# Bulk loads of adjacent rows, and bulk results that leave in runs of 8 bytes instead of 32

## The chip, the cores and the metric

One Trainium2 chip, one core in use. The metric is the device time of one execution in microseconds (us); medians of several executions are given. In the profile a packet is one unbroken run of bytes that one of the core's 16 DMA engines moves. A pitch is the distance in memory from one partition's piece to the next one's. A store's receipt is the time from its last packet to its landing.

## The reference

For a float32 matrix of 8192 x 8192 (268 MB) the largest absolute value of each row:

```python
def reference(x):                       # x: 8192 x 8192 float32
    return np.linalg.norm(x, ord=np.inf, axis=1)
```

Every element is read once and compared once; the output is 8192 floats, 32 KB. The kernel is therefore a load stream with a reduction behind it.

## The kernel before

The rows are divided into a bulk (48 rows for each of the 128 partitions) and a tail (16 rows for each). In the bulk, each load brings `B` = 2 rows to each partition: 128 x 64 KB = 8 MB. Three buffers take turns.

```python
G: int = 4, B: int = 2, BUFS: int = 3
# ...
A = n_bulk_rows // (G * B)              # 48 // 8 = 6
x_b = x[:split].rearrange("(a p n b) c -> a n p (b c)", p=P, a=A, n=G, b=B)
out_b = out[:split].rearrange("(a p n b) -> p a (n b)", p=P, a=A, n=G, b=B)
# ...
r_bulk = outp.tile([P, A, G * B], F32)
# ...
for a in range(A):
    for n in range(G):
        t = sbuf.tile([P, W + PAD], F32, tag="t")
        nc.sync.dma_start(out=t[:, :W], in_=x_b[a, n])
        absmax(r_bulk[:, a, n * B : (n + 1) * B],
               t[:, :W].rearrange("p (b c) -> p b c", b=B))
# ... the tail: loads of falling size, 21 and then 13, each with its reduction ...
    if j == len(LAST) - 4:              # late in the tail
        ins = nc.scalar.dma_start(out=out_b, in_=r_bulk[:])   # the bulk store
        after(ins, done, mybir.DependencyClass.Sync)
nc.sync.dma_start(out=out_t, in_=r_tail[:])                   # the last store
```

With `G` = 4, a partition owns 8 neighbouring rows in each of 6 groups and reads two of them in each load. Its 8 results are neighbours in the output, so the bulk store moves 128 x 6 = 768 runs of 32 bytes.

## Time and profile before

| | before |
|---|---|
| median time | 627.68 us (627.46 to 627.82, 3 runs) |
| span in the profile | 625.7 us |
| DMA engines | full in all 40 slices but the end |
| last load packet ends | 622.66 us |
| bulk store: issued, landed | 621.73, 623.73 us |
| last store: issued, landed | 624.05, 625.47 us |

"Landed" is the moment at which the store's completion counter has its last increment. The lines themselves stand in the prediction below.

### The profile page before, as it was taken

The numbers are of one execution on the slowest core, as the hardware profiler recorded it, in microseconds if no ns is written. First come the engines' busy times: TensorE is split into PE (matmuls) and PEld (weight loads), VectorE is DVE, ScalarE is ACT, GpSimd is POOL, SyncE is SP. The second block draws the span as 40 slices with busy tenths as digits, with TensorE's granted clock in tenths as the row PEclk, the third lists the DMA queues.
The fourth block names the chain that finished last, engine by engine and source line by source line (L and its number), as shares of the span: only waits on it lengthen the run. The fifth ranks groups of instructions, "written<-read, shape, count | busy, mean of one in ns | idle before, by whom it ended". The sixth has DMA issues, their size and how long they took to land.

```text
span 625.7 us, 205 instructions
## 1 busy us (share of the span) xinstructions
DVE 552.9 (88%) x67; POOL 0.2 (0%) x4
## 2 busy tenths in 40 slices
DVE  0588988889988889888898888988889999999998
POOL 0000000000000000000000000000000000000000
DMA  9999999999999999999999999999999999999997
GB/s 402 469 402 452 419 452 419 448 423 436 436 419 452 411 461 402 469 402 469 402 469 402 461 411 452 419 448 423 444 413 421 444 425 431 436 425 430 424 422 315
DMA packets 9282, 268.49 MB, mean 429 GB/s; under 512 B 1856, under 2 KB 1856, under 8 KB 3392
## 3 DMA queue, kind: packets, MB, share of 16 engines
q1 hardware_dynamic: 8496, 268.45, 99.5%
q10 hardware_dynamic: 784, 0.02, 0.1%
q14 instruction: 2, 0.02, 0.0%
HBM read 268.44 MB, written 0.03 MB: 429 GB/s over the span
## 4 chain that ended last, share of the span: by engine, by line
DMA 67%; DVE 31%; issue 1%; another core or an unknown queue 0%; DVEq 0%; SPq 0%
DMA t<-in_x_dram 67%; DVE r_bulk L140 24%; DVE part L140 6%; DVE t L140 2%; DVEq L230 0%; DVE r_tail L140 0%; SPq L159 0%
## 5 line engine op out<-in xcount | busy, mean ns | idle before, releaser
L140 DVE TENSOR_REDUCE r_bulk<-t 128x2 f32<-128x16384 f32 x24 | 413.3, 17220 | 69.7 <-DMA t<-in_x_dram 69.7
L140 DVE TENSOR_REDUCE part<-t 128x1 f32<-128x8192 f32 (+20 forms) x28 | 121.5, 4410 | 0.3 <-DMA t<-in_x_dram 0.3
L140 DVE TENSOR_REDUCE t<-t 128x1 f32<-128x1664 f32 (+8 forms) x11 | 16.7, 1576 | 0.2 <-DMA t<-in_x_dram 0.2
L140 DVE TENSOR_REDUCE r_tail<-t 128x1 f32<-128x644 f32 (+1 forms) x2 | 1.5, 814 | 0.0
L137 DVE MEMSET part<- 128x56 f32 x1 | 0.1, 105 | 0.9 <-PEq L219 0.9
L140 DVE TENSOR_REDUCE r_tail<-part 128x14 f32<-128x56 f32 x1 | 0.2, 201 | 0.0
L219 POOL MEMSET const-bfloat16-1.0<- 128x1 bf16 x1 | 0.1, 101 | 0.0
L219 POOL MEMSET const-uint8-127<- 128x1 uint8 x1 | 0.1, 101 | 0.0
L219 POOL MEMSET const-float32-0.0<- 128x1 f32 x1 | 0.1, 98 | 0.2 <-issue 0.2
L219 POOL MEMSET const-float32-1.0<- 128x1 f32 x1 | 0.1, 98 | 0.0
## 6 DMA issues: line engine op xcount, KB each, us to landing
t<-in_x_dram SPq DMA_DIRECT2D x2, 3392.0 KB, 37.2
t<-in_x_dram SPq DMA_DIRECT2D x1, 5376.0 KB, 40.5
t<-in_x_dram SPq DMA_DIRECT2D x1, 4864.0 KB, 32.9
t<-in_x_dram SPq DMA_DIRECT2D x1, 4800.0 KB, 32.9
t<-in_x_dram SPq DMA_DIRECT2D x1, 4672.0 KB, 34.7
t<-in_x_dram SPq DMA_DIRECT2D x3, 1536.0 KB, 36.9
t<-in_x_dram SPq DMA_DIRECT2D x1, 3520.0 KB, 42.7
t<-in_x_dram SPq DMA_DIRECT2D x1, 3328.0 KB, 40.4
```

What stands on the lines that cost most here:

```text
L137: nc.vector.memset(part[:], 0.0)
L140: return nc.vector.reduce_max(out=o, in_=i, axis=X, apply_absolute_value=True)
L219: nc = _bacc.Bacc("TRN2", target_bir_lowering=False, num_devices=1)
```

## The change

The intent is to let each bulk load read one unbroken stretch of 8 MB, where before its 128 pieces of 64 KB lay 256 KB apart. The price is in the output: a partition then owns only 2 neighbouring rows in each of 24 groups.

```diff
-    G: int = 4,
+    G: int = 1,
```

So `A` becomes 24, and the bulk store moves 128 x 24 = 3072 runs of 8 bytes. Nothing else changes, neither in the order of instructions nor in their waits.

## The prediction

> **What bounds the kernel now.** I read the page's head and slices first, to see which resource is full; then the same question in equal windows, to see whether it is full in every stage; then the groups of instructions, for what the other engine has to spare; then the chain that ended last and the timeline of the last four microseconds, because the change also touches a store that sits there.
>
> The page of the kernel before, head, slices and queues (share of the span for each engine; tenths busy and GB/s in 40 slices; packets, MB and share of the 16 DMA engines for each queue):
>
> ```profile
> span 625.7 us, 205 instructions
> DVE 552.9 (88%) x67; POOL 0.2 (0%) x4
> ...
> DMA  9999999999999999999999999999999999999997
> ...
> DMA packets 9282, 268.49 MB, mean 429 GB/s; under 512 B 1856, under 2 KB 1856, under 8 KB 3392
> q1 hardware_dynamic: 8496, 268.45, 99.5%
> q10 hardware_dynamic: 784, 0.02, 0.1%
> ```
>
> The DMA engines are full from the first slice to the last; VectorE, the only computing engine, is at 88%. Queue 1 (all loads, and the small last store) takes 99.5% of 16 engines' time. Queue 10 is the bulk store: 784 packets, 24 KB, 0.1%. So the load stream is the bound, and its rate is the question.
>
> The equal windows (us, then VectorE busy, POOL busy, clock, DMA share, GB/s): two in the bulk stage, two in the tail of smaller loads.
>
> ```profile
> 136.00:194.00 58.00, 51.66 (x3) 0.00 (x0) 1.00 1.00 434
> 368.00:426.00 58.00, 51.66 (x3) 0.00 (x0) 1.00 1.00 434
> 500.00:560.00 60.00, 59.71 (x11) 0.00 (x0) 1.00 0.99 427
> 560.00:610.00 50.00, 49.97 (x19) 0.00 (x0) 1.00 1.01 427
> ```
>
> Every 58 us brings three bulk loads, at 434 GB/s, with the DMA engines never idle. VectorE has 58.00 - 51.66 = 6.3 us of slack in each such window, which is the idle time of the first group here:
>
> ```profile
> L140 DVE TENSOR_REDUCE r_bulk<-t 128x2 f32<-128x16384 f32 x24 | 413.3, 17220 | 69.7 <-DMA t<-in_x_dram 69.7
> ```
>
> A reduction takes 17.22 us where a load takes 58.02 / 3 = 19.34 us. In the queue's own waits each of these loads waits for the reduction that frees its buffer (361.6 us over 21 waits), but two loads are always queued ahead, so these waits cost the stream nothing: the DMA share in the windows is 1.00.
>
> The packet records give the rate in its parts. All 3072 bulk packets are 64 KB, one for each partition of each load, at a median of 2418 ns: 65536 / 2418 = 27.1 GB/s for an engine, 434 for 16. Eight packets for each engine in each load make 8 x 2.418 = 19.34 us, exactly the load's period. Small load packets of 2560 bytes take 102 ns. A line through both sizes is 7.8 ns + bytes / 27.2 GB/s, and it also gives the sizes between (26112 bytes: 968 ns both measured and by the line). So the rate of a packet is set by a fixed 27.2 GB/s for an engine and a few ns for each packet.
>
> The end, from the chain that ended last (start, length, what) and from the timeline:
>
> ```profile
> 612.35 9.89 DVE t L140 x8
> 622.25 0.23 issue
> 622.48 0.59 DVE r_tail L140
> ```
>
> ```profile
> 621.73 0.41 ACTq L200 DMA_DIRECT2D out_dram<-r_bulk  x1
> 622.48 1.55 DVE L140 TENSOR_REDUCE r_tail<-t 128x1 f32<-128x644 f32 x2
> 624.05 0.35 SPq L202 DMA_DIRECT2D out_dram<-r_tail  x1
> ```
>
> The last load packet ends at 622.66. The last reduction ends at 624.03, the last store is issued at 624.05, and its packets run from 624.89 to 625.10 in the packet records. The page's list of issues has it landing 1.4 us after issue, at 625.47; the span ends at 625.73. The bulk store is issued at 621.73, its first packet is at 622.69 (after nearly all load packets), its last at 623.21, and it has landed 2.0 us after issue, at 623.73. It is off the end by 625.47 - 623.73 = 1.74 us.
>
> **What the Trainium skill says.** "DMA: Bandwidth & Descriptors", section "Where 436 GB/s comes from", gives 16 ports x 32 bytes x 850 MHz = 435.2 GB/s on the SBUF side. The trace's 434 in the bulk stage is within 0.4% of it, so the case agrees: the ceiling is where the data is written, not in the order in which HBM is read.
>
> The same page, "Latency and other measured facts", reports that copies between HBM tensors slow down at large power-of-two pitches between partitions: 207 GB/s at 512 KiB against 214 at full rate, 164 at 2 MiB. It recommends laying tiles out contiguously. That is the likely intent here. This trace shows no loss to recover: 256 KB pitch in the bulk and 512 KB in the tail (8 segments of 64 KB for each partition) lie on the same line of ns against bytes.
>
> The same page, "Measured (HBM→SBUF, 128 partitions, SWDGE, issued from GpSimd)", puts the smallest packets at about 10.5 ns each. Here the bulk store's 49 packets on an engine took 0.52 us, 10.6 ns each, though on another issuing path.
>
> **The change, part by part.** With G = 1 the number of bulk steps is 48 rows / (1 x 2) = 24 where it was 6 groups of 4. The number of loads, their size, their order on the queue, their waits and the reductions stay: the ordering tool shows no difference on SyncE or VectorE. Two things change.
>
> (1) Load addresses. Each partition still reads one 64 KB run, so packets remain 3072 of 64 KB; only the pitch between partitions falls from 256 KB to 64 KB. By the line above this is worth 0. What could be gained at most: raising 434 to the page's 435.2 over the bulk's 465 us is 465 x 0.0034 = 1.6 us, and about half of the difference is the fixed ns for each packet, which stays; the mean bulk packet is 2422 ns against a median of 2418, so stalls that a better pattern could remove are 4 x 8 x 24 ns = 0.8 us, nearly all of it in the first load (mean 2497 ns), where the start-up is. I count 0, with 0.3 us either way.
>
> (2) The bulk store. Its runs in HBM were 8 results = 32 bytes; they become 2 results = 8 bytes. Packets with data go from 768 to 3072, that is from 48 to 192 for each engine. Added engine time: 144 x 10.8 ns (0.52 us / 48) = 1.56 us. Issue: the store with 48 data packets for an engine took 0.41 us to issue, the last store with 8 took 0.35, so about 1.65 ns for each packet; 144 more make about 0.24 us, of which some may delay the first packet. All this comes after the last loads have been read, so it doesn't delay them. It first fills the slack: last packet at 622.69 + 192 x 0.0108 = 624.77, or 625.01 with the whole issue delay; receipts took 0.35 to 0.51 us after the last packet before, so it lands between 625.1 and 625.5. The last store lands at 625.47 now. So the bulk store arrives just about when the last store does. Where the two overlap (624.89 on), each engine has a few packets more to take turns with, 0.1 to 0.2 us. Sum: 1.56 + 0.24 + 0.2 = 2.0 us of added work, of which 1.74 us is slack; the end moves by 0 to 0.5 us. I take 0.3.
>
> Total: 627.68 + 0 + 0.3 = 628.0 us.
>
> **The rivals.** (a) HBM locality makes the loads faster. For it: adjacent rows, and the skill's advice. Against it: every engine already moves 27.1 GB/s with no idle time. It can give 1 us at most: 626.7.
>
> (b) The adjacent pattern makes the loads slower, because at a 64 KB pitch the engines running in step meet in the same HBM channels. For it: nothing in this trace, only that 64 KB is also a power of two. Against it: 256 and 512 KB show no such loss, and the new pattern as a whole covers one unbroken range. If packets became 1% slower in the bulk, the load stream would add 4.7 us: 632. VectorE's slack means that no second bound appears.
>
> (c) The 8-byte writes cost more than 10.8 ns each, because several partial writes fall into the same line of memory, or because ACT's queue cannot produce descriptors that fast. For it: 32-byte writes had receipts up to 0.51 us after the last packet, 64-byte ones 0.21 to 0.37. Against it: the packets themselves last 7 to 9 ns whatever their size up to 64 bytes. At twice the cost a packet the store would land 2.1 us later than reckoned, near 627.4, and the time would be 629.7.
>
> (d) The store starts earlier and hits the loads. It cannot: its wait, on the reduction before it, is not moved.
>
> **Range and chances.** The step from which the range comes is (2): from nothing visible (627.3, with the usual scatter of 0.2 us and a trace of (a)) to a store half again as slow (629.3). A change by 2% is 12.6 us. Up, it needs packets of the bulk 2.7% slower, which only (b) gives; down, it would need more than 435 GB/s. Chances: faster 0.01, same 0.97, slower 0.02.
>
> **What would show it.** In the changed kernel's page: 11586 packets in all (9282 + 2304), those of queue 10 3088 where 784 were; the bulk windows again 58 us for three loads at 434 GB/s; 64 KB packets again at 2418 ns; the bulk store landing about 3.5 us after its issue (2.0 + 1.56) and the last store still 1.4 to 1.6. The span should be 625.7 to 626.2. The prediction is wrong if the windows in the bulk show another rate (rivals a and b), or if the bulk store lands over 4.5 us after issue, so that the end waits for it alone (rival c).

## The result, and the profile after

The changed kernel took 634.18 us (633.47 to 634.91, 5 runs) against 627.56 us (627.37 to 627.82, 5 runs): a ratio of 1.0105, 95% interval 1.0091 to 1.0119. A ratio is the mean time of one kernel's fast runs over that of the other's in the same rounds, so not quite the ratio of the medians. The prediction was 628.0 us with a range up to 629.3: wrong by 6 us, though within 2% as it said.

First the page of the changed kernel, the same parts as were shown of the kernel before:

```profile
span 631.6 us, 205 instructions
DVE 553.0 (88%) x67; POOL 0.2 (0%) x4
...
DMA  9999999999999999999999999999999999999994
...
DMA packets 11586, 268.49 MB, mean 425 GB/s; under 512 B 4160, under 2 KB 4160, under 8 KB 5696
...
q1 hardware_dynamic: 8496, 268.45, 98.6%
q10 hardware_dynamic: 3088, 0.02, 0.2%
```

The packet counts are those predicted. The first 39 slices are as full as before; only the last digit fell, from 7 to 4. So the loss is in the last 16 us. Two of the bulk windows (us, then VectorE busy, POOL busy, clock, DMA share, GB/s) confirm that the loads are not it:

```profile
136.00:194.00 58.00, 51.66 (x3) 0.00 (x0) 1.00 1.00 434
368.00:426.00 58.00, 51.66 (x3) 0.00 (x0) 1.00 1.00 434
```

Now the end, cut into windows of 1 us (same columns):

```profile
622.00:623.00 1.00, 1.00 (x2) 0.00 (x0) 1.00 0.28 41
623.00:624.00 1.00, 1.00 (x2) 0.00 (x0) 1.00 0.75 14
624.00:625.00 1.00, 0.07 (x1) 0.00 (x0) 1.00 0.34 6
625.00:626.00 1.00, 0.00 (x0) 0.00 (x0) 1.00 0.21 7
626.00:627.00 1.00, 0.00 (x0) 0.00 (x0) 1.00 0.15 4
627.00:628.00 1.00, 0.00 (x0) 0.00 (x0) 1.00 0.00 0
...
630.00:631.00 1.00, 0.00 (x0) 0.00 (x0) 1.00 0.00 0
```

VectorE is done at 624.07. The last data packet of a store is over at 627.11, and the last record of the 4-byte packets that count it as done at 627.47; from there to the end nothing is busy at all: no engine, no DMA packet. The program waits. The timeline of the changed kernel and its list of DMA issues (last number: us from issue to landing) say for what:

```profile
621.77 0.41 ACTq L200 DMA_DIRECT2D out_dram<-r_bulk  x1
622.52 1.55 DVE L140 TENSOR_REDUCE r_tail<-t 128x1 f32<-128x644 f32 x2
624.09 0.35 SPq L202 DMA_DIRECT2D out_dram<-r_tail  x1
```

```profile
out_dram<-r_bulk ACTq DMA_DIRECT2D x1, 24.0 KB, 9.3
out_dram<-r_tail SPq DMA_DIRECT2D x1, 8.0 KB, 7.3
```

The same two lines of the kernel before:

```profile
out_dram<-r_bulk ACTq DMA_DIRECT2D x1, 24.0 KB, 2.0
out_dram<-r_tail SPq DMA_DIRECT2D x1, 8.0 KB, 1.4
```

Every step up to the issue of the last store comes within 0.05 us of the kernel before (624.09 against 624.05). Then the bulk store, issued at 621.77, lands at 631.12 instead of 623.73, and the last store lands 0.25 us after it, at 631.37 instead of 625.47. These 5.90 us are the whole difference between the two spans (631.63 and 625.73). The packet records split the bulk store's landing in two: its packets run from 622.76 to 626.67, 20 ns each on an engine where they took 10.8 before, and the last counter increment comes 4.45 us after the last packet, where it came 0.52 us after before. The last store is a victim: its data packets ended at 627.11, but its counter waited.

The Trainium skill, "DMA: Bandwidth & Descriptors", section "Queues, rings and completion order", says that the increment of a completion counter is a strongly ordered write, which lands only after every earlier write from that DMA engine, on whichever queue. The trace agrees: in every run with a slow bulk store at the end, the last store's landing stands 0.15 to 0.4 us behind the bulk store's (0.25 us in the changed kernel). Having its own queue did not make it independent. No run separates this order from a memory that is merely busy with the earlier writes.

One trap in reading: the chain of work that ended last stops, in both kernels, at VectorE's end near 624.1. In the changed kernel the 7.5 us between that and the end of the span are in none of its lines. A wait for writes to land, at the very end, shows in the list of issues and in the windows, not in the chain.

### The profile page after: what moved, and what is told of

It reads as the page before. It is cut to its first block, busy times and chain, and to the rows that moved or that the text cites. A ratio compares the mean times of both kernels' runs of the same rounds, so it can differ in the third digit from the quotient of the medians.

```text
span 631.6 us, 205 instructions
## 1 busy us (share of the span) xinstructions
DVE 553.0 (88%) x67; POOL 0.2 (0%) x4
## 2 busy tenths in 40 slices
DMA packets 11586, 268.49 MB, mean 425 GB/s; under 512 B 4160, under 2 KB 4160, under 8 KB 5696
## 3 DMA queue, kind: packets, MB, share of 16 engines
q10 hardware_dynamic: 3088, 0.02, 0.2%
## 4 chain that ended last, share of the span: by engine, by line
DMA 64%; DVE 33%; issue 1%; another core or an unknown queue 0%; DVEq 0%; SPq 0%
DMA t<-in_x_dram 64%; DVE r_bulk L140 24%; DVE part L140 7%; DVE t L140 3%; DVEq L230 0%; SPq L159 0%; DVE r_tail L140 0%
```

## The experiments

Theory S: neighbouring short writes share a line of memory, and what costs is that they wait for each other. Theory W: a write under some size costs its DMA engine a fixed time wherever it goes. Theory L: part of the loss is in the addresses of the loads. "First packet to landing" below runs from the bulk store's first packet to its last counter increment; it is 8.36 us in the changed kernel and 1.04 us in the kernel before. It comes from one profiled execution of each run. The runs that store to scratch at the end, the one in order and the one with 768 runs had one round each: two executions, which lie within 0.5 us.

### Loads or store?

The new loads with the old store (results in a wrong order):

```diff
-    out_b = out[:split].rearrange("(a p n b) -> p a (n b)", p=P, a=A, n=G, b=B)
+    out_b = out[:split].rearrange("(a p n b) -> p a (n b)", p=P, a=6, n=4, b=B)
...
-            ins = nc.scalar.dma_start(out=out_b, in_=r_bulk[:])
+            ins = nc.scalar.dma_start(out=out_b, in_=r_bulk[:].rearrange("p (a g) c -> p a (g c)", a=6))
```

> Adjacent 8 MB loads as in the changed kernel, bulk store in the old 768 runs of 32 bytes (the results leave in a wrong order, on purpose). Theory (the whole loss is the store's slow landing): same as before, 627.2 to 628.0, bulk store landing about 2.0 us after issue. Rival (part of the loss is in the loads' addresses): 629 or more.

628.37 us against 627.70, ratio 1.0011 (0.9997 to 1.0026). The bulk store landed in 2.0 us, as before. The time is 0.4 us above what was expected, which is taken up again further down.

The old loads with the new store (`G` = 4, and 24 runs of 2 in the output pattern; wrong order):

> Old loads at a pitch of 256 KB, bulk store in 3072 runs of 8 bytes (wrong order, on purpose). Theory: as slow as the changed kernel, 633.5 to 635, bulk store landing about 9 us after issue. Rival (loads' addresses carry part): clearly less than 633.

633.58 us against 627.70, ratio 1.0093 (1.0078 to 1.0108). Its list of issues:

```profile
out_dram<-r_bulk ACTq DMA_DIRECT2D x1, 24.0 KB, 9.1
out_dram<-r_tail SPq DMA_DIRECT2D x1, 8.0 KB, 7.1
```

The store alone brings the loss, with the same landing. Theory L is not needed for it.

### How much for half the runs?

`G: int = 2`: 1536 runs of 16 bytes, results right.

> Two load groups instead of one or four (G = 2): pitch 128 KB, bulk store in 1536 runs of 16 bytes, results right. Theory (writes land at a fixed rate, in the changed kernel 3072 in some 8.2 us, 2.7 ns each): 1536 land in 4.1 us after the first packet at 622.7, the last store behind them: span about 627.3, time 629.2. Rival (the cost comes from 8-byte size alone, below some size): as before, 627.7.

628.29 us, ratio 1.0009 (0.9994 to 1.0024); the bulk store landed 4.1 us after issue. That is half a miss: from first packet to landing it took 3.12 us, not the 4.1 of a fixed rate by count. Per write of an engine (3.12 us / 96) it is 33 ns, where the changed kernel has 8.36 / 192 = 44. So the size or the neighbours of a write matter too, and with 3.1 us the store still fits its slack nearly.

### Size of a run, or neighbours in one line?

Each run of 8 bytes to its own 512 bytes of a scratch tensor (bulk results missing from the output):

```diff
-    out_b = out[:split].rearrange("(a p n b) -> p a (n b)", p=P, a=A, n=G, b=B)
+    scr = nc.dram_tensor("scr", [A, P, 128], F32, kind="Internal").ap()
+    out_b = scr[:, :, : G * B].rearrange("a p c -> p a c")
```

> The changed kernel, but its 3072 runs of 8 bytes go to a scratch tensor in HBM at a pitch of 512 bytes, so that no two of them touch the same 512 bytes (the bulk results are missing from the output, on purpose). Theory S (what costs is that neighbouring small writes share a line of memory and wait for each other): landing 3 to 4.5 us after issue, time 627.7 to 629. Rival W (each write under some size costs its DMA engine 40 to 49 ns wherever it goes): landing 8 to 9.5 us after issue, 633 to 635.

629.97 us, between the two expectations: the store landed 5.8 us after issue. Neighbours are part of the cost, not all of it.

The opposite: the 24 runs of a partition next to each other, kept apart by gaps in the source (wrong order):

```diff
-    out_b = out[:split].rearrange("(a p n b) -> p a (n b)", p=P, a=A, n=G, b=B)
+    out_b = out[:split].rearrange("(p a n b) -> p a (n b)", p=P, a=A, n=G, b=B)
...
-    r_bulk = outp.tile([P, A, G * B], F32)
+    r_bulk = outp.tile([P, A, 2 * G * B], F32)
...
-            ins = nc.scalar.dma_start(out=out_b, in_=r_bulk[:])
+            ins = nc.scalar.dma_start(out=out_b, in_=r_bulk[:, :, : G * B])
```

> The changed kernel, with the 24 runs of a partition written next to each other, 192 bytes in a row (still 3072 writes of 8 bytes, made separate by gaps in the source; order of results wrong, on purpose). Theory S (sharing of a line): worse than the changed kernel, or at least as slow, 634 to 640, because the neighbours now follow each other directly. Rival W (cost by write): as the changed kernel, 633 to 635. If it is fast (under 630), what counts is neighbours written by different engines, or the 1 KB step between writes that follow each other.

639.75 us, the slowest of all, ratio 1.0193 (1.0172 to 1.0213). Its list of issues:

```profile
out_dram<-r_bulk ACTq DMA_DIRECT2D x1, 24.0 KB, 14.6
out_dram<-r_tail SPq DMA_DIRECT2D x1, 8.0 KB, 12.4
```

The same count of the same size costs 5 us more when the neighbours of a line follow each other directly. This is what theory S says. (The gapped source is a second difference; the issue itself also took 0.60 us instead of 0.41.)

The same count with runs of 32 bytes, packed without gaps in 96 KB of scratch (bulk results missing):

```diff
-    out_b = out[:split].rearrange("(a p n b) -> p a (n b)", p=P, a=A, n=G, b=B)
+    scr = nc.dram_tensor("scr", [A, P, 8], F32, kind="Internal").ap()
+    out_b = scr[:, :, :].rearrange("a p c -> p a c")
...
-    r_bulk = outp.tile([P, A, G * B], F32)
+    r_bulk = outp.tile([P, A, 8], F32)
+    nc.vector.memset(r_bulk[:], 0.0)
```

> The changed kernel, with 3072 runs of 32 bytes (96 KB) to a scratch tensor in the same order (bulk results missing from the output, on purpose). If the count of writes sets the cost (42 ns each for an engine): landing 8 to 9.5 us after issue, 633 to 635. If the size of a run sets it (32 bytes: 12 ns, as in the kernel before): 192 x 12 = 2.3 us of packets, landing about 3.8 us after issue, 627.7 to 628.5.

628.29 us, ratio 1.0010 (0.999 to 1.003). Its list of issues:

```profile
scr<-r_bulk ACTq DMA_DIRECT2D x1, 96.0 KB, 3.7
out_dram<-r_tail SPq DMA_DIRECT2D x1, 8.0 KB, 1.6
```

Four times the bytes of the changed kernel in as many writes, and it costs next to nothing. So the count of writes alone is not the cause. Nor is it ACT's queue, which gives out as many writes here as in the changed kernel. Its packets took 1.88 us and it landed 0.9 us after the last: this is nearly the store that the prediction described (192 packets at 10.8 ns, landing about 3.5 us after issue).

Two more runs ask how large the line is. They are the scratch run again, with a pitch of 32 and of 64 bytes in place of 512 (`[A, P, 8]` and `[A, P, 16]`, 8 bytes used in each; bulk results missing):

> The run with a scratch tensor, at a pitch of 32 bytes in place of 512: 3072 runs of 8 bytes, each the first 8 of its own 32 bytes, two of them in each 64 (bulk results missing from the output, on purpose). If memory's unit is 32 bytes: as at 512 bytes, landing 5.8 us after issue, 630. If it is 64 bytes, two writes share a unit, as in the half version with 16-byte runs in fours: clearly slower, landing 7 us or more, 631 to 633. If larger: as the changed kernel, 633 to 635.

> The same at a pitch of 64 bytes: one write in each 64 bytes (bulk results missing from the output, on purpose). If memory's unit is 32 or 64 bytes: landing 5.8 us after issue, 630. If it is larger than 64: slower, 631 or more.

At 32 bytes: 631.62 us, landing 7.1 us after issue. At 64 bytes: 630.09 us, landing 5.7. The list of issues of the run at 64 bytes:

```profile
scr<-r_bulk ACTq DMA_DIRECT2D x1, 24.0 KB, 5.7
out_dram<-r_tail SPq DMA_DIRECT2D x1, 8.0 KB, 3.6
```

All runs with 3072 writes at the end, by how they share 64 bytes:

| runs | in one 64 bytes | first packet to landing |
|---|---|---|
| 32 bytes | 2, filling it | 2.78 us |
| 8 bytes, own 512 | 1 | 4.86 us |
| 8 bytes, own 64 | 1 | 4.74 us |
| 8 bytes, own 32 | 2 | 6.19 us |
| 8 bytes, the changed kernel | 8 | 8.36 us |
| 8 bytes, in order | 8, one after the other | 13.3 us |

From 512 to 64 bytes hardly anything changes; from 64 to 32 it costs 1.45 us. So short writes get in each other's way at 32 bytes from start to start and not at 64: a unit of 64 bytes fits these runs. Runs of 32 bytes share 64 bytes too and pay nothing for it: being short and sharing go together. The runs at own 32 bytes start at the same places as those of 32 bytes and differ in length alone: 6.19 against 2.78 us. No run has 32 bytes alone in their 64, so length and filling the 64 bytes are not separated there. What memory does inside no run shows.

### Is it the number of them?

Only 6 of the 24 bulk steps are stored: 768 runs of 8 bytes, eight to each 64 bytes (the other results missing).

```diff
-            ins = nc.scalar.dma_start(out=out_b, in_=r_bulk[:])
+            ins = nc.scalar.dma_start(out=out_b[:, :6], in_=r_bulk[:, :6])
```

> The changed kernel storing only 6 of its 24 bulk steps: 768 runs of 8 bytes, eight to each 64 bytes as in the changed kernel (the other bulk results missing from the output, on purpose). If each write costs its engine about 42 ns from the first on: 48 x 42 = 2.0 us from first packet, plus 0.4 for the receipt, landing 3.4 us after issue, just at the last store: 627.5 to 628.3. If the cost comes only once many writes are under way: landing about 2.0 us after issue as for 768 runs of 32 bytes. If the writes wait for the memory of a few lines, which now hold a quarter: a quarter of 8.4 us, as the first.

629.20 us against 627.64, ratio 1.0025 (1.0005 to 1.0045); landing 4.2 us after issue. That is above all three expectations. Half of the time lost is not the store's: in the profiled run the loads ended 0.8 us later than before (623.46 against 622.66), and the last store landed 2.25 us after its issue instead of 1.42. The packets themselves took 0.55 us, as those of 32 bytes did; the landing came 2.7 us after the last. So 768 runs of 8 bytes took 3.26 us from first packet to landing where 768 of 32 bytes took 1.04. So 768 of them are not free either, and a quarter of the writes took more than a quarter of the time (8.36 us). The packet times do not show the cost.

### An early store: a theory that fell

If the writes are only slow to land, storing earlier should hide them. The bulk store of the changed kernel moves up to where the last bulk reduction ends, near 484 us:

```diff
+    nc.scalar.dma_start(out=out_b, in_=r_bulk[:])
+
     def after(ins, first, kind):
...
-        if j == len(LAST) - 4:
-            ins = nc.scalar.dma_start(out=out_b, in_=r_bulk[:])
-            after(ins, done, mybir.DependencyClass.Sync)
```

> The changed kernel with its bulk store issued as soon as the last bulk reduction ends, near 484 us, among loads. Theory (the engines only hand the writes on, and what is slow is their landing): the loads give up little, 627.7 to 629.5. Rival (a small write holds its DMA engine, 192 x 20 to 42 ns): the load stream is delayed by 4 to 8 us, 631.5 to 635.5.

635.33 us, ratio 1.0120 (1.0103 to 1.0137): slower still. I took it for a cost of each write to its engine, 7.6 us / 192 = 40 ns, and tested that with three more early stores: runs of 32 bytes (the kernel before), 8 bytes to own 512 bytes, and 3072 runs of 32 bytes (the last two to scratch).

> The kernel before (768 runs of 32 bytes), with its bulk store issued early, near 484 us, among the loads. If in the early store of the changed kernel each of the 192 turns between the two queues cost 49 ns whatever is written: 48 x 49 = 2.4 us, 630. If the 8-byte write itself costs it: at 12 ns, 0.6 us, 628.2 or less.

> The early store of the changed kernel (8-byte runs among loads, which cost 49 ns a write), but to own 512 bytes each (bulk results missing from the output, on purpose). If sharing of a unit of memory was what cost there: 627.7 to 629. If a write of 8 bytes among loads costs its engine 49 ns wherever it goes: 635 to 636. In between: both play a part.

> The early store with 3072 runs of 32 bytes to a scratch tensor (bulk results missing from the output, on purpose). If the 8 bytes were what cost 29 ns a write among loads: at most the 10 ns of a packet, 192 x 10 = 1.9 us, 627.5 to 629.5. If the count of turns between the queues costs it, whatever is written: 633, as with 8 bytes on own lines.

They gave 627.82, 633.18 and 632.38 us against 627.63, 627.52 and 627.64. The last rules out the 8 bytes as the main cause here, and left "192 turns between two queues cost 25 ns each". But windows of the early 8-byte store, with the columns as above, do not lose time where the store's packets run (488 to 553 us):

```profile
545.00:550.00 5.00, 5.00 (x3) 0.00 (x0) 1.00 1.01 434
550.00:555.00 5.00, 5.00 (x2) 0.00 (x0) 1.00 0.65 177
555.00:560.00 5.00, 5.00 (x1) 0.00 (x0) 1.00 0.16 37
560.00:565.00 5.00, 1.72 (x1) 0.00 (x0) 1.00 0.93 371
```

Up to 550 the load stream is whole; then it runs dry, with 37 GB/s left. SyncE's own waits in the same trace (who waited for whom; us in total, times, longest):

```profile
SPq L159 <- DMA out_dram<-r_bulk: 39.3, 1, 39.3
```

The order of the built program explains it: a load of the tail was to use the same completion counter as the store (eight are handed out in turn), so SyncE held it back until the store had landed, and with it all loads behind it. That load was issued at 558.54, the store landed at 558.52. Why so late, 74.1 us after issue? Up to 550 us each engine had moved 57 of the store's 192 packets beside 51 load packets: about one for one, 1.1 us a turn. The other 135 were still waiting, and nearly all of them went between 552 and 553.4, when no load packets were left. So the loads held back the store, and then the store held back the loads.

The size of the loss fits too. In the 8-byte store, the one to own 512 bytes and the one with 3072 runs of 32 bytes, SyncE's wait for the store was 39.3, 36.3 and 35.3 us, and the profiled spans are 9.4, 5.7 and 4.7 us longer than before. With 768 runs of 32 bytes it waited 24.0 us and lost nothing. So loads already queued covered some 30 us of such a wait, and each microsecond above that was lost. So both my readings of the early store were wrong: neither the 8 bytes nor the turns cost the DMA engines anything like this; they only delayed a landing, and a queue waited for that.

A last kernel tests this reading: the same 3072 runs of 8 bytes, results right, in six stores of 4 bulk steps, each issued as its results come, so that each should have landed before its counter is wanted, or soon after.

```diff
-    r_bulk = outp.tile([P, A, G * B], F32)
+    S = 4
+    r_bulk = [outp.tile([P, S, G * B], F32, name=f"r_bulk{s}") for s in range(A // S)]
...
+        if a % S == S - 1:
+            nc.scalar.dma_start(out=out_b[:, a - S + 1 : a + 1], in_=r_bulk[a // S][:])
```

> The changed kernel with the same 3072 runs of 8 bytes, but stored in six parts of 4 bulk steps, each as soon as its results are there (5 among the bulk loads, the last near 484 us); results right. Each part takes 32 turns with 64 KB load packets of 2.42 us, so it has landed some 80 us after issue, about 20 us before a load wants its counter. If the loss of the early store was this wait: at most a packet's 10 ns x 192 = 1.9 us, 627.6 to 629.8. If the 8-byte writes cost the DMA engines 29 to 40 ns each: 633 to 635.5.

629.03 us against 627.67, ratio 1.0019 (1.0002 to 1.0035), within what was expected. The waits and the list of issues:

```profile
SPq L162 <- DMA out_dram<-r_bulk: 17.7, 2, 11.3
```

```profile
out_dram<-r_bulk ACTq DMA_DIRECT2D x6, 4.0 KB, 74.7
out_dram<-r_tail SPq DMA_DIRECT2D x1, 8.0 KB, 1.4
```

Two loads still waited for a counter, 17.7 us in all, but with enough loads queued ahead: the windows from 545 to 560 us are at 0.97 to 1.01. The last store is back at 1.4 us. With the 8-byte runs kept, about 5 of the 6.6 us are gone. The 1.4 us left are in the load stream: in the profiled run the loads end at 623.80 instead of 622.66. They are within the estimate of 192 packets at 10 ns; how much of them is that and how much scatter stays open.

### A repair, and longer runs

Adjacent loads, results right, and the short runs gone: after the last bulk reduction VectorE turns the results in 32x32 blocks, so that they leave in 96 runs of 256 bytes.

```diff
-    r_bulk = outp.tile([P, A, G * B], F32)
+    r_bulk = outp.tile([P, B, 32], F32)
+    turned = outp.tile([P, 32, B], F32)
...
+    for b in range(B):
+        nc.vector.transpose(out=turned[:, :, b], in_=r_bulk[:, b, :])
+    for i in range(4):
+        nc.scalar.dma_start(
+            out=out_b[i],
+            in_=turned[32 * i : 32 * i + A].rearrange("p c b -> p (c b)"),
+        )
```

> A repair, results right: adjacent loads of the changed kernel; after the last bulk reduction VectorE turns the bulk results in blocks of 32x32 (2 instructions), so that they leave in 96 runs of 256 bytes, near 484 us. Theory (adjacent loads are neutral, short writes were the whole loss): 627.3 to 628.3, as before. Rival (adjacent loads cost a little, as the 628.4 of the run with the loads alone may hint): 628.3 or more in all rounds.

628.17 us against 627.52, ratio 1.0009 (0.9994 to 1.0024): repaired, but not better than the kernel before. (The stores were issued at 507.2 us and not near 484, because VectorE did four reductions of the tail before the two turns.) And `G: int = 8` (loads 512 KB apart, 384 runs of 64 bytes, results right):

> Eight load groups (G = 8): loads at a pitch of 512 KB, bulk store in 384 runs of 64 bytes, results right. If the end of the kernel before is set by the last store and not by the bulk store: no gain, 627.2 to 628.2. If pitch mattered after all: slower.

628.23 us against 627.64, ratio 1.0010 (0.9995 to 1.0025). No gain: the bulk store landed 1.7 us after issue, and the end is the last store's in either case. Its bulk windows are at 434 GB/s too. No version beat the kernel before.

### Do the loads cost half a microsecond?

Several kernels with another pitch came out about 0.6 us above the kernel before, each time within the noise of a comparison. So the kernel before ran again under another label, beside the run with only the loads changed, in five rounds:

> The kernel before, unchanged, run as if it were a changed one. If the 0.6 us belongs to the loads: 627.4 to 627.8, as the kernel before. If it belongs to how runs follow each other: 628.2 or so.

> Adjacent loads, old store in runs of 32 bytes (wrong order, on purpose), as once before, in more rounds. If the loads cost 0.6 us: 628.0 to 628.5 where k_same has 627.6. If they are neutral: within 0.3 us of k_same.

627.52 us (ratio 0.9998, 0.9986 to 1.0011) and 628.14 us (1.0005, 0.9992 to 1.0019). The five runs of the adjacent loads were 627.46, 627.49, 628.14, 628.20 and 628.62; the kernel before had such values in the same rounds too (627.62 to 628.26). The profiled run with adjacent loads ended its loads at 622.54, the one of the kernel before at 622.59. Where a run is above, its trace shows single loads, most of them among the first nine, with packets of 2430 to 2490 ns instead of 2419, in the kernel with the old pitch and the new store as well (2458 ns in its seventh load; its loads ended at 623.62). So no cost of the loads is shown. One under 0.2% is not ruled out, and it stays a little suspicious that all such comparisons fell on the same side.

## Why the prediction was wrong

**Right: the bound, and part (1).** The load stream sets the time up to 622.7 us, its rate is 434 GB/s with pitches of 64, 128, 256 and 512 KB alike, and the adjacent rows bring no gain. Rivals (a) and (b) did not occur, and (d) was rightly ruled out: the store's issue did not move.

**Right: the counts, and the slack.** Packets were 11586 and 3088, and all up to the issue of the last store stayed in place within 0.05 us.

**Wrong: the cost of the store in part (2).** The step that failed is "Added engine time: 144 x 10.8 ns (0.52 us / 48) = 1.56 us", with the receipt then taken over from before ("receipts took 0.35 to 0.51 us after the last packet before"). The price of a packet was measured on 32-byte runs and carried to 8-byte runs. Measured: the packets took 3.39 us more (3.91 against 0.52) where 1.56 was reckoned, the receipt 4.45 us where 0.35 to 0.51 was, and the landing came at 631.12 where 625.1 to 625.5 was. The 0.24 us for a longer issue did not come at all: the issue took 0.41 us as before. The sign that the prediction named for this, a landing over 4.5 us after issue, appeared: 9.3 us. The mechanism, a store that outgrows its slack of 1.74 us, was the right one; its size was not. The runs give the terms: 2.78 us for as many writes of 32 bytes (this the working had right), 2.0 us more for runs of 8 bytes that share no 64 bytes (4.74), 3.6 us more where eight share them (8.36).

**Right in kind, dismissed on weak evidence: rival (c).** It named partial writes into the same line. The argument against it was that "the packets themselves last 7 to 9 ns whatever their size up to 64 bytes". That is still true in the changed kernel (7.5 ns for a packet of 8 bytes), and it says nothing: the cost lies between packets and after them. Even (c) was sized too small, at twice the cost of a packet. Its other reason, descriptors that ACT's queue cannot produce fast enough, did not hold: the same queue moved 3072 runs of 32 bytes at 9.8 ns each on an engine.

**Missing: the coupling of the stores.** The prediction saw the two stores meet only in "a few packets more to take turns with, 0.1 to 0.2 us". In fact the last store's landing moved with the bulk store's, from 1.4 to 7.3 us after issue. This miss cost little by itself: with the bulk store landing at 631.12, the coupling put only 0.25 us on the end.

## What to carry to other kernels

When a layout is changed for the loads, look at what it does to the runs of the stores: here runs of 8 bytes, eight to each 64 bytes, cost 6 us at the end, for 24 KB. Price a store by its landing in the list of issues, not by its packet times, and don't carry a packet's price from one size of run to another. Before moving a slow store forward, see which later transfers share its completion counter: an early store that lands late can stop the load queue.

## What the Trainium skill lacked or had wrong

- "DMA: Bandwidth & Descriptors", "Specifications": it puts the size below which writes are read, modified and written back at 512 bytes. No run here writes 512 bytes at once, so that limit is not tested. What the page lacks is a further step below it: from first packet to landing, 384 runs of 64 bytes took 0.77 us, 768 of 32 took 1.04 and 3072 of 32 took 2.78, but 3072 runs of 8 bytes took 4.74 without sharing.
- No page has the cost of short writes that share a line: 3072 runs of 8 bytes took 4.74 us with one in each 64 bytes, 6.19 with two, 8.36 with eight, and 13.3 with eight one after the other.
- The same page, "Measured (HBM→SBUF, 128 partitions, SWDGE, issued from GpSimd)": its 10.5 ns a packet is close to the 32-byte writes here (9.8 and 10.8 ns), but not to the 8-byte writes of the changed kernel (20 ns), and the landing is not in it: there the last increment came 4.45 us after the last packet.
- The same page, "Latency and other measured facts", has a loss at a pitch of 512 KiB for copies within HBM (207 GB/s of 214). For these loads into SBUF no run shows one: 434 GB/s at 64, 128, 256 and 512 KB.
- No page has a number for how late a store among loads can land (74.1 us, at about 1.1 us a packet on each engine while loads were queued), or warns that a later transfer on the same completion counter then waits (39.3 us).
